# First MLP of a two-layer encoder step: hidden rows loaded one group ahead, and the conditioning of layer 1 in eight narrow and twelve wide steps

## The chip, the cores and the metric

One NeuronCore of a Trainium2 chip runs the kernel. TensorE (PE) multiplies matrices into eight PSUM banks of 128 x 512 f32, VectorE (DVE) and ScalarE (ACT) work on tiles of 128 partitions in SBUF and read PSUM, GpSimd (POOL) does little here, and SyncE (SP) issues the DMAs, which 16 DMA engines carry out. The metric is the device time of one execution in microseconds (us); less is better.

## The reference, cut to what matters

Two layers of an encoder work on 1024 prompt tokens and 32 sample tokens of width 1024. Each layer is a mixer and an MLP, each followed by a layer norm. Shifts, scales and gates (6 x 1024 a layer, and 2 x 1024 for the shared keys and values) come from a conditioning vector c for the prompt and another for the samples:

```python
def ada_mod(c, w, b):
    return jax.nn.silu(c) @ w + b
...
kv_shift, kv_scale = jnp.split(ada_mod(c, p['w_ada_kv'], p['b_ada_kv'])[:, None, :], 2, axis=-1)
...
x = layer_norm(ALPHA * x + (1 + g1) * y, p['ln_g'][l, 0], p['ln_b'][l, 0])
u = x * (1 + sc2) + sh2
f = jnp.square(jax.nn.relu(u @ p['w_up'][l])) @ p['w_down'][l]
x = layer_norm(ALPHA * x + (1 + g2) * f, p['ln_g'][l, 1], p['ln_b'][l, 1])
```

All is f32. The first MLP (layer 0) turns u (1056 tokens x 1024) into h (4096 wide) and that into f. What follows it is layer 1: q from the modulated x, then keys, values and attention.

## The kernel before, in words

Every f32 operand of a matmul is split into a high and a low part (fp32r, `split`, L89 on ACT and L90 on DVE), and a product is three matmuls (high x high, high x low, low x high: L118, L119, L120). Tokens lie along the free dimension, T = 1056, in three blocks `TBS` of 384, 384 and 288, or in four quarters `QN` of 264.

**Up.** `mlp7(L0)` first makes h. The 16 column blocks pb of w_up are worked on in `jobs`, a pair (pb, half of the tokens): 22 jobs of seven products each, 154 in all, and a product is 12 matmuls of 264 columns (`Seven.product`, L1269), evicted by ACT and DVE into H. `h_forms` squares and splits H (tile HL) and stores it to DRAM (`hpl`, L1136). The weights of a job come by `forms`: two raw tiles of 512 KB (rdn_u), four sums and eight splits on DVE and ACT. Raw tiles come from a ring of three buffers (tag raw, `raw_tile`), in which the weights of down (raw_dn) and the narrow conditioning data (rada) stand as well.

**Down.** h has 32 row blocks of 128, in eight groups g of four. A group takes four weight tiles pr (`w_plain`: raw_dn, split into w_dn), each for two column blocks fc of the output, and for each fc all token blocks: `dn_plain`, 12 matmuls into one PSUM bank, then an eviction by DVE that adds the gated product to the accumulator ACX (L1034). The part of a block that holds sample tokens is evicted on its own. Groups 0 to 6 go by fc, group 7 by token block, and after each of its blocks `L0.after` starts the layer norm of that block (`norm`, tasks n01_0 to n01_2). h of a group is loaded back by `h_load` (L1326, L1330), four tiles of 1056 KB: group 0 into half the tokens of U, whose contents are no longer needed, group 1 into four tiles hs of a pool f4 that takes the place of the H and HL tiles, group 2 into the other half of the tokens of U, and so on in turn. Where h lies in U in strips (groups 0, 2, 3, 5, 6), matmuls go by quarters of 264; in groups 1, 4 and 7 by TBS. `h_load(g + 2)` is called behind the second to fourth weight tile of group g.

**Conditioning beside the MLP.** Layer 1's conditioning is made by DVE while PE multiplies: for each slice of w_ada, 8 row blocks times a scalar of silu(c), for the prompt and for the samples, summed up (`aacc`, `aw`), then a transpose (`aat`, `awt`), a reduction (`cx`), and after every fourth narrow or second wide step a tiny matmul `adas`. `ada_cols` does it in narrow steps of two columns of 128 (two loads rada of 512 KB, 16 operations of 128 x 256, L238 and L241), `ada_wide` in wide steps of four (two loads radw of 1 MB into the ring wc of six buffers, where the split weights w_dn stand too; 16 operations of 128 x 512, L265 and L267). Both are generators: a `Flow` steps them by a nominal time, `flow.tick` is called after each product of up (QN / pace) and each block of down (n / 192), and a `yield x` asks for the next call after x. Up runs `ada_some`: 4 narrow steps for the first half of w_ada_kv at pace 480. Down runs `ada_rest`: 12 wide steps of w_ada[1], 2 wide steps of the second half of w_ada_kv, then the small `ada_fix` and `combine`, and `bias_table`. `L0.after` finishes all that is left (`flow.finish(norms["ada"])`) before it starts a norm.

**What sets the order.** The calls say what depends on what; a scheduler then fixes the order of each engine's instructions and of SP's DMAs, and at run time each engine takes its instructions strictly in that order. An order within an engine that was good for the scheduler's own guess of the times is kept whatever the real times are.

At pace 480 a product counts 264 / 480 = 0.55, so a narrow step with `ADA_B` = (4, 2, 1, 8) takes 8 + 4 products for each half and 2 at the end, 26; the fourth has 15 at its end, and they are done with product 3 x 26 + 24 + 15 = 117. At pace 320 a product counts 0.825, and a step takes 2 x (5 + 3) + 2 = 18; eight of them, with 10 at the end of the fourth and the eighth, come to 160, more than the 154 there are.

## Time and profile before

| | us |
|---|---|
| median of 3 runs | 2483.89 |
| the profiled execution | 2483.62 |
| its span, first to last instruction | 2481.8 |
| PE busy in the span | 2367.8 |
| DVE busy | 1994.5 |
| ACT busy | 1179.6 |

Times in the profile are counted from the start of the span. Up's seven products run from about 640 to 862 us; groups 0 to 7 of down begin at 862.2, 919.6, 966.5, 1013.4, 1060.5, 1107.3, 1154.2 and 1201.1; the first matmul of q is at 1295.14. PE's busy time counts a matmul until its modelled end, so PE can be busy without being at its peak. Where a line says `<-`, the name behind it is what the instruction waited for.

### The profile page before, as it was taken

How to read it: one execution, taken by the hardware profiler on the slowest of the kernel's cores; microseconds unless marked ns; L12 is line 12 of the kernel's file. 1: busy time of each engine (PE TensorE's matmuls, PEld its weight loads, DVE VectorE, ACT ScalarE, POOL GpSimd, SP SyncE). 2: the span in 40 equal slices, each digit the busy share in tenths (PEclk: the TensorE clock that was granted, in tenths of full speed). 3: DMA queues.
4: the chain of work that ended last, by engine and by line, in shares of the span. 5: the costliest groups of instructions: out<-in, count | busy, mean ns of one | idle time of the engine just before them, and what ended most of it. 6: DMA issues, size and time to landing. Idle time of an engine off the chain costs nothing.

```text
span 2481.8 us, 45295 instructions
## 1 busy us (share of the span) xinstructions
PE 2367.8 (95%) x17564; PEld 2274.1 (92%) x17564; DVE 1994.5 (80%) x4254; ACT 1179.6 (48%) x2394; POOL 167.0 (7%) x315
## 2 busy tenths in 40 slices
PE   7999999999999989999939989999999999899997
PEld 4999999999999989999939978779999999899997
DVE  4899999788787779998398666764998888888778
ACT  4644456487566611111038456762776777322212
POOL 0211100000000000000000224430000000000003
PEclk9999999999999999999969999999999999999999
DMA  8433224346556896574231330033376779966642
GB/s 295 123 109 101 84 88 131 115 136 210 181 191 226 300 349 234 202 243 138 88 101 65 98 79 1 10 79 77 123 267 226 256 255 344 368 234 239 227 163 71
DMA packets 298556, 423.68 MB, mean 171 GB/s; under 512 B 15832, under 2 KB 222060, under 8 KB 295268
## 3 DMA queue, kind: packets, MB, share of 16 engines
q1 hardware_dynamic: 298340, 420.78, 50.7%
q8 instruction: 138, 2.26, 0.4%
q14 instruction: 78, 0.64, 0.1%
HBM read 304.91 MB, written 118.17 MB: 170 GB/s over the span
## 4 chain that ended last, share of the span: by engine, by line
PE 46%; DVE 13%; DMA 5%; ACT 4%; issue 2%; SPq 1%; POOL 0%; DVEq 0%; ACTq 0%; POOLq 0%
PE dn L1407 11%; PE up L1269 5%; PE dn L120 5%; PE dn L118 5%; PE dn L119 5%; PE pv L1838 3%; PE s L1781 2%; PE pt L1816 2%; DVE wf_u L90 2%; DMA rdn_u<-in_w_up_dram 1%; PE q L118 1%; DVE HL L90 1%; PE q L119 1%; PE q L120 1%; PE op_b L118 1%
## 5 line engine op out<-in xcount | busy, mean ns | idle before, releaser
L1034 DVE SCALAR_TENSOR_TENSOR ACX<-dn,ada,ACX 128x264 f32<-128x264 f32 (+6 forms) x696 | 288.5, 437 | 122.9 <-PE dn L120 74.2
L1407 PE MATMUL dn<-fx,wf_d 128*128 128x264 f32 x2016 | 255.1, 286 | 6.1 <-DVE ACX L1034 3.8
L1407 PEld LDWEIGHTS dn<-fx,wf_d 128*128 128x128 f32 x2016 | 249.9, 189 | 8.1 <-DVE ACX L1034 2.4
L118 PE MATMUL dn<-U,w_dn 128*128 128x264 f32 x640 | 183.9, 287 | 6.0 <-DVE ACX L1034 6.0
L119 PE MATMUL dn<-U,w_dn 128*128 128x264 f32 x640 | 182.8, 286 | 0.0
L120 PE MATMUL dn<-U,w_dn 128*128 128x264 f32 x640 | 181.0, 285 | 1.5 <-DVE w_dn L90 1.5
L89 ACT CAST w_dn<-raw_dn 128x1024 fp32r<-128x1024 f32 x36 | 37.6, 1050 | 281.1 <-PE dn L120 125.3
L1269 PE MATMUL up<-TF,wf_u 128*128 128x264 f32 x1056 | 143.3, 285 | 2.1 <-ACT H L1272 2.1
L265 DVE SCALAR_TENSOR_TENSOR aw<-radw,cs,aw 128x512 f32<-128x512 f32 x196 | 138.9, 745 | 7.9 <-DMA radw<-in_w_ada_dram 7.9
L1269 PE MATMUL up<-u,wf_u 128*128 128x264 f32 x1056 | 139.6, 285 | 1.3 <-ACT wf_u L89 0.6
L1269 PE MATMUL up<-U,wf_u 128*128 128x264 f32 x1056 | 139.6, 285 | 1.1 <-ACT H L1272 0.5
L1269 PEld LDWEIGHTS up<-TF,wf_u 128*128 128x128 f32 x1056 | 134.2, 188 | 3.0 <-ACT H L1272 2.7
L1269 PEld LDWEIGHTS up<-U,wf_u 128*128 128x128 f32 x1056 | 133.1, 188 | 2.2 <-DVE H L1275 1.4
L1269 PEld LDWEIGHTS up<-u,wf_u 128*128 128x128 f32 x1056 | 132.6, 188 | 1.9 <-ACT wf_u L89 0.8
L118 PE MATMUL dn<-hs,w_dn 128*128 128x384 f32 (+2 forms) x416 | 131.9, 317 | 0.0
L119 PE MATMUL dn<-hs,w_dn 128*128 128x384 f32 (+2 forms) x416 | 131.3, 316 | 0.0
L120 PE MATMUL dn<-hs,w_dn 128*128 128x384 f32 (+2 forms) x416 | 130.7, 314 | 0.0
L118 PEld LDWEIGHTS dn<-U,w_dn 128*128 128x128 f32 x640 | 121.7, 190 | 6.4 <-DVE ACX L1034 6.2
L120 PEld LDWEIGHTS dn<-U,w_dn 128*128 128x128 f32 x640 | 120.3, 189 | 2.0 <-DVE w_dn L90 2.0
L119 PEld LDWEIGHTS dn<-U,w_dn 128*128 128x128 f32 x640 | 122.1, 191 | 0.0
L238 DVE SCALAR_TENSOR_TENSOR ada_room<-ada_room,cs 128x256 f32<-128x256 f32 x224 | 99.7, 480 | 3.3 <-DMA ada_room<-in_w_ada_dram 3.3
L120 PE MATMUL up<-u,w_up 128*128 128x264 f32 x320 | 92.4, 290 | 3.0 <-DVE w_up L90 3.0
(394 smaller groups left out, 7161.9 us busy)
## 6 DMA issues: line engine op xcount, KB each, us to landing
hpl<-HL SPq DMA_DIRECT2D x144, 264.0 KB
rdn_u<-in_w_up_dram SPq DMA_DIRECT2D x64, 512.0 KB
hd<-HL SPq DMA_DIRECT2D x28, 1056.0 KB
fx<-hd SPq DMA_DIRECT2D x50, 528.0 KB
radw<-in_w_ada_dram SPq DMA_DIRECT2D x24, 1024.0 KB
hd<-HM SPq DMA_DIRECT2D x28, 792.0 KB
U<-hpl SPq DMA_DIRECT2D x40, 528.0 KB
raw_up<-in_w_up_dram SPq DMA_DIRECT2D x40, 512.0 KB
```

Of the source, the lines that this page charges most:

```text
L90: (eng or nc.vector).tensor_sub(dst_l, src, dst_h.bitcast(F32))
L118: nc.tensor.matmul(ps, wh, mov(0, k), start=(k == 0), stop=False)
L119: nc.tensor.matmul(ps, wh, mov(1, k), start=False, stop=False)
L120: nc.tensor.matmul(ps, wl, mov(0, k), start=False, stop=(k == nk - 1))
L238: nc.vector.scalar_tensor_tensor(acc[:, cnd], raw[:, k], sc, acc[:, cnd], op0=ALU.mult, op1=ALU.add)
L265: nc.vector.scalar_tensor_tensor(acc[cnd], raw[:, k], sc, acc[cnd], op0=ALU.mult, op1=ALU.add)
L1034: nc.vector.scalar_tensor_tensor(xs, ps[:, off + o:off + o + mm_], gate[:, fc, cnd:cnd + 1], xs, op0=ALU.mult, op1=ALU.add)
L1269: nc.tensor.matmul(p, self.ws[w][:, wl, k], moving(f, tp, xl, k), start=first and k + n_ == 0, stop=k == 3 and n_ == 2, skip_group_check=n ...
L1407: nc.tensor.matmul(p, ws[w][:, wl, k], t[:, s0, xl], start=first and k + n_ == 0, stop=k == kg - 1 and n_ == 2, skip_group_check=not first)
L1781: nc.tensor.matmul(s[:, b, :w], qst, kk[i][:, g, k0 + j0:k0 + j0 + w], start=(i == 0), stop=(i == 1))
L1816: nc.tensor.transpose(pt[:kp, j - j0, pr * P:(pr + 1) * P], ps_[pr][:, j * P:j * P + kp], ident)
L1838: nc.tensor.matmul(pv[64 * e:64 * e + 64, :nq], V[:kp, vt0 + j, g * 64:(g + 1) * 64], pts[e][:kp, j, :nq], start=(j == 0), stop=(j == nt - 1))
```

## The change

- Groups 1 to 7 all go by TBS. Odd groups have h in the tiles of f4, even groups from 2 on in `L.half(c)`, the high half of U over all tokens; group 0 keeps its strips. `h_load(g + 1)` is called in group g, behind its first weight tile, for all four tiles at once; before it was `h_load(g + 2)`.
- `ada_some` has 8 narrow steps (all of w_ada_kv) at pace 320, `ada_rest` 12 wide ones. A wide step calls for the next half's load before it works on its own half, and yields (5, 5, 2) instead of (6, 3, 3).
- The norm of block 2 has shorter waits.

```diff
--- before.py
+++ after.py
@@ -251,22 +251,33 @@
 
     def ada_wide(src, c0, base, nch, mk, tmp_f, raw_f, step):
 
-        for j in range(0, nch, 4):
-            acc = [tmp_f([P, 512], f"aw_{base}_{j}_{cnd}") for cnd in range(2)]
-            for half in range(2):
-                raw = raw_f([P, 4, 512], f"radw_{base}_{j}_{half}")
-                nc.sync.dma_start(raw, src[512 * half:512 * half + 512, c0 + j * P:c0 + (j + 4) * P].rearrange(
+        jobs = [(j, half) for j in range(0, nch, 4) for half in range(2)]
+        raws = {}
+
+        def load(i):
+            if i < len(jobs):
+                j, half = jobs[i]
+                raws[i] = raw_f([P, 4, 512], f"radw_{base}_{j}_{half}")
+                nc.sync.dma_start(raws[i], src[512 * half:512 * half + 512, c0 + j * P:c0 + (j + 4) * P].rearrange(
                     "(k p) c -> p k c", p=P))
-                yield step[0]
-                for k in range(4):
-                    for cnd in range(2):
-                        sc = cs[:, 4 * half + k, cnd:cnd + 1]
-                        if half or k:
-                            nc.vector.scalar_tensor_tensor(acc[cnd], raw[:, k], sc, acc[cnd], op0=ALU.mult, op1=ALU.add)
-                        else:
-                            nc.vector.tensor_scalar(acc[cnd], raw[:, k], sc, None, op0=ALU.mult)
-                    if k == 1:
-                        yield step[1]
+        load(0)
+        yield step[0]
+        for i, (j, half) in enumerate(jobs):
+            load(i + 1)
+            raw = raws.pop(i)
+            if not half:
+                acc = [tmp_f([P, 512], f"aw_{base}_{j}_{cnd}") for cnd in range(2)]
+            for k in range(4):
+                for cnd in range(2):
+                    sc = cs[:, 4 * half + k, cnd:cnd + 1]
+                    if half or k:
+                        nc.vector.scalar_tensor_tensor(acc[cnd], raw[:, k], sc, acc[cnd], op0=ALU.mult, op1=ALU.add)
+                    else:
+                        nc.vector.tensor_scalar(acc[cnd], raw[:, k], sc, None, op0=ALU.mult)
+                if k % 2:
+                    yield step[k // 2]
+            if not half:
+                continue
             for cnd in range(2):
                 at = tmp_f([P, 512], f"awt_{base}_{j}_{cnd}")
                 nc.vector.transpose(at, acc[cnd])
@@ -859,11 +870,11 @@
         return acc
 
     ADA_B = (4.0, 2.0, 1.0, 8.0)
-    ADA_W = (6.0, 3.0, 3.0)
+    ADA_W = (5.0, 5.0, 2.0)
     NOW = True
     TAIL = (1.0, 1.5)
     W00 = (6.0, 12.0, 0.0, 0.0, 0.0, 3.0)
-    W01 = (6.0, 12.0, 3.0, 3.0, 3.0)
+    W01 = ((6.0, 12.0, 3.0, 3.0, 3.0), (3.0, 6.0, 0.0, 0.0, 0.0))
     W10 = ((10.0, 12.0, 0.0, 0.0, 0.0, 3.0), (16.0, 14.0, 0.0, 0.0, 0.0, 3.0))
 
     def make_layer(acc, pp, uo, cut=None):
@@ -1321,16 +1332,13 @@
         def h_load(g, c, hl=None):
 
             src = hpl[4 * order_p[g] + c]
-            if g % 3 == 1:
-                t = f4p.tile([P, 2, T], F32R, tag=f"f4{c}", name=f"hs_{l}_{g}_{c}")
-                nc.sync.dma_start(t.bitcast(F32), src)
-                hs_p[g, c] = lambda hl, t0, n: t[:, hl, t0:t0 + n]
+            if hl is not None:
+                nc.sync.dma_start(L.strips(2 * c + hl).bitcast(F32), src[:, hl].rearrange("p (h t) -> p h t", h=2))
+                hs_p[g, c] = lambda hl, t0, n: L.strips(2 * c + hl)[:, t0 // (2 * QN), t0 % (2 * QN):t0 % (2 * QN) + n]
                 return
-            for i in range(2) if hl is None else (hl,):
-                nc.sync.dma_start(L.strips(g % 3 // 2, 2 * c + i).bitcast(F32),
-                                  src[:, i].rearrange("p (h t) -> p h t", h=2))
-            hs_p[g, c] = lambda hl, t0, n: L.strips(g % 3 // 2, 2 * c + hl)[:, t0 // (2 * QN),
-                                                                            t0 % (2 * QN):t0 % (2 * QN) + n]
+            t = f4p.tile([P, 2, T], F32R, tag=f"f4{c}", name=f"hs_{l}_{g}_{c}") if g % 2 else L.half(c)
+            nc.sync.dma_start(t.bitcast(F32), src)
+            hs_p[g, c] = lambda hl, t0, n: t[:, hl, t0:t0 + n]
 
         def dn_plain(g, fc, t0, n):
             ps = mm(f"dn{l}_{g}_{fc}_{t0}")
@@ -1458,11 +1466,11 @@
                 if g < 7:
                     for pr in range(4):
                         w_plain(g, pr)
-                        if g < 6 and pr:
-                            for c in ((0, 1), (2,), (3,))[pr - 1]:
-                                h_load(g + 2, c)
+                        if g and pr == 0:
+                            for c in range(4):
+                                h_load(g + 1, c)
                         for fc in (2 * pr, 2 * pr + 1):
-                            for t0, n in TBS if g % 3 == 1 else blocks_p:
+                            for t0, n in TBS if g else blocks_p:
                                 dn_plain(g, fc, t0, n)
                 else:
                     for pr in range(4):
@@ -1560,11 +1568,10 @@
     h_cm.__exit__(None, None, None)
 
     def ada_some():
-        yield from ada_cols(a["w_ada_kv"], 0, 96, 8, mm, tmp_t, ADA_B)
+        yield from ada_cols(a["w_ada_kv"], 0, 96, 16, mm, tmp_t, ADA_B)
 
     def ada_rest():
         yield from ada_wide(a["w_ada"][1], 0, 48, 48, mm, tmp_t, wc_tile, ADA_W)
-        yield from ada_wide(a["w_ada_kv"], D, 104, 8, mm, tmp_t, wc_tile, ADA_W)
         ada_fix(48, [(1, "sc"), (2, "g"), (4, "sc"), (5, "g")])
         ada_fix(96, [(1, "sc")])
         combine(1, lng(1), lnb(1), ada_part(1, 1), ada_part(1, 0))
@@ -1574,7 +1581,7 @@
 
     class L0:
         wups = wup0
-        l, nw, pace, alloc, add, gate = 0, 0, 480, mm, add_gated_at, ada_part(0, 5)
+        l, nw, pace, alloc, add, gate = 0, 0, 320, mm, add_gated_at, ada_part(0, 5)
         blocks = TBS
         pairs, quarters = (0, 1), (0, 1, 2, 3)
         first = FIRST
@@ -1593,9 +1600,13 @@
             t0 = (2 * tp + q) * QN
             return L0.rows(4 * kap, 4, hl)[:, :, t0:t0 + QN]
 
-        def strips(tp, i):
-
+        def strips(i):
+
+            tp = L0.pairs[0]
             return L0.rows(2 * i % KC, 2, 2 * i // KC)[:, :, 2 * tp * QN:2 * (tp + 1) * QN]
+
+        def half(c):
+            return L0.rows(2 * c, 2, 0)
 
         def scratch(i):
             t = accp0.tile([P, 2, 2, KG, QN], F32R, tag=f"acc{i}", name=f"TF0_{i}")
@@ -1619,7 +1630,7 @@
             t0, n = blk
             ti = TBS.index(blk)
             flow.finish(norms["ada"])
-            norms[ti] = flow.add(norm(ti, 1, f"n01_{ti}", W01, False, lambda ti: acc_dma(
+            norms[ti] = flow.add(norm(ti, 1, f"n01_{ti}", W01[ti == 2], False, lambda ti: acc_dma(
                 xsp[1][:, :, t0:t0 + n], acc[ti], True)), now=NOW)
     mlp7(L0)
```

What this does to the order, at three places. In the rows below dn_g_fc_t names a block of down (group, column block, first token), radw_48_j_half a wide load, aw_104 the wide steps of w_ada_kv, n01_0 the norm of block 0, and the last numbers only count tiles.

SP in group 0, before:

```order
L96 DMA raw_dn0_0_2_10665<-in_w_down_dram 128x4x256
L96 DMA raw_dn0_0_3_10800<-in_w_down_dram 128x4x256
L1609 DMA ACX0_1_10391<-xsp3_80 128x2112 x2
L1136 DMA hpl0_6125<-HL0_15_1_10325 256x1x264 x4
L258 DMA radw_48_0_0_10431<-in_w_ada_dram 128x4x512
L1330 DMA U_134<-hpl0_6125 128x2x528
L1136 DMA hpl0_6125<-HL0_13_1_10394 256x1x264 x4
L1330 DMA U_134<-hpl0_6125 128x2x528 x2
L1326 DMA hs_0_1_0_10407<-hpl0_6125 128x2112
L1326 DMA hs_0_1_1_10409<-hpl0_6125 128x2112
L1326 DMA hs_0_1_2_10411<-hpl0_6125 128x2112
L1326 DMA hs_0_1_3_10413<-hpl0_6125 128x2112
```

and now:

```order
L261 DMA radw_48_0_0_10531<-in_w_ada_dram 128x4x512
L261 DMA radw_48_0_1_10590<-in_w_ada_dram 128x4x512
L1147 DMA hpl0_6125<-HL0_13_1_10490 256x1x264 x4
L261 DMA radw_48_4_0_10716<-in_w_ada_dram 128x4x512
L1340 DMA hs_0_1_0_10509<-hpl0_6125 128x2112
L1340 DMA hs_0_1_1_10511<-hpl0_6125 128x2112
L1340 DMA hs_0_1_2_10513<-hpl0_6125 128x2112
L1340 DMA hs_0_1_3_10515<-hpl0_6125 128x2112
L96 DMA raw_dn0_0_2_10765<-in_w_down_dram 128x4x256
L96 DMA raw_dn0_0_3_10902<-in_w_down_dram 128x4x256
L96 DMA raw_dn0_1_0_11031<-in_w_down_dram 128x4x256
```

The third and fourth weights of group 0 (raw_dn0_0_2, raw_dn0_0_3) stood ahead of the last stores of h, and now stand behind the four tiles of h of group 1.

DVE in group 7, before (block 2's evictions, the two wide steps, the norm of block 0):

```order
L1034 SCALAR_TENSOR_TENSOR ACX0_0_9705<-dn0_7_3_768_14367,ada_88,ACX0_0_9705 128x256
L1034 SCALAR_TENSOR_TENSOR ACX0_0_9705<-dn0_7_3_768_14367,ada_88,ACX0_0_9705 128x32
L267 TENSOR_SCALAR aw_104_0_0_13995<-radw_104_0_0_13997,cs_87 128x512
...
L274 TENSOR_REDUCE cx_118<-awt_104_0_1_14090 128x2x8
L267 TENSOR_SCALAR aw_104_4_0_14093<-radw_104_4_0_14095,cs_87 128x512
L267 TENSOR_SCALAR aw_104_4_1_14094<-radw_104_4_0_14095,cs_87 128x512
L265 SCALAR_TENSOR_TENSOR aw_104_4_0_14093<-radw_104_4_0_14095,cs_87,aw_104_4_0_14093 128x512
...
L274 TENSOR_REDUCE cx_118<-awt_104_4_1_14118 128x2x8
L915 TENSOR_TENSOR s_n01_0_14152<-ACX0_0_9705 128x768
L288 TENSOR_TENSOR ada_88<-adas_104_6_14121,pt2_86 128x16
L917 TENSOR_TENSOR s_n01_0_14152<-s_n01_0_14152,ACX0_1_10391 128x768
```

and now:

```order
L1045 SCALAR_TENSOR_TENSOR ACX0_1_10487<-dn0_7_6_0_13704,ada_88,ACX0_1_10487 128x384
L1045 SCALAR_TENSOR_TENSOR ACX0_1_10487<-dn0_7_7_0_13718,ada_88,ACX0_1_10487 128x384
L928 TENSOR_TENSOR s_n01_0_13732<-s_n01_0_13732,ACX0_1_10487 128x768
L929 TENSOR_TENSOR s_n01_0_13732<-s_n01_0_13732 128x384
L1045 SCALAR_TENSOR_TENSOR ACX0_0_9762<-dn0_7_0_384_13740,ada_88,ACX0_0_9762 128x384
L90 TENSOR_TENSOR sr_n01_0_13737<-s_n01_0_13732,sr_n01_0_13737 128x384
L1045 SCALAR_TENSOR_TENSOR ACX0_0_9762<-dn0_7_2_384_13768,ada_88,ACX0_0_9762 128x384
L936 TENSOR_TENSOR ACX0_0_9762<-ACX0_0_9762,mean_n01_0_13782 128x2x384 x2
L936 TENSOR_TENSOR ACX0_1_10487<-ACX0_1_10487,mean_n01_0_13782 128x2x384 x2
L940 TENSOR_TENSOR q0_n01_0_13786<-q0_n01_0_13786,q2_n01_0_13789 128x768
```

The norm's sums (s_n01_0) stood behind both wide steps and behind evictions of block 2 (tokens from 768); now they stand among the last evictions of block 0, ahead of those of block 1 (tokens from 384).

DVE at the end of up, before (H0_13 and H0_15 are evictions of the last two jobs, which PE waits for; wf_u0_13 is a weight split):

```order
L1275 TENSOR_TENSOR H0_13_1_10234<-up0_13_1_1_10262,H0_13_1_10234 128x264
L90 TENSOR_TENSOR w_dn0_0_0_10278<-raw_dn0_0_0_10276,w_dn0_0_0_10278 128x1024
L1275 TENSOR_TENSOR H0_15_1_10103<-up0_15_1_2_10215,H0_15_1_10103 128x264
L90 TENSOR_TENSOR wf_u0_13_6_10295<-rdn_u0_13_1_10059,wf_u0_13_6_10295 128x512
L90 TENSOR_TENSOR w_dn0_0_1_10348<-raw_dn0_0_1_10346,w_dn0_0_1_10348 128x1024
L1275 TENSOR_TENSOR H0_13_1_10234<-up0_13_1_0_10235,H0_13_1_10234 128x264
L90 TENSOR_TENSOR HL0_15_1_10325<-H0_15_1_10103,HL0_15_1_10325 128x4x264
```

and now:

```order
L1286 TENSOR_TENSOR H0_13_1_10319<-up0_13_1_1_10347,H0_13_1_10319 128x264
L1286 TENSOR_TENSOR H0_15_1_10178<-up0_15_1_2_10300,H0_15_1_10178 128x264
L238 SCALAR_TENSOR_TENSOR aacc_96_14_10129<-rada_96_14_1_10298,cs_87,aacc_96_14_10129 128x256 x8
L245 STREAM_TRANSPOSE aat_96_14_10439<-aacc_96_14_10129 128x512
L90 TENSOR_TENSOR w_dn0_0_0_10363<-raw_dn0_0_0_10361,w_dn0_0_0_10363 128x1024
L90 TENSOR_TENSOR wf_u0_13_6_10384<-rdn_u0_13_1_10134,wf_u0_13_6_10384 128x512
L90 TENSOR_TENSOR HL0_15_1_10414<-H0_15_1_10178,HL0_15_1_10414 128x4x264
L246 TENSOR_REDUCE cx_118<-aat_96_14_10439 128x16
L1286 TENSOR_TENSOR H0_13_1_10319<-up0_13_1_0_10320,H0_13_1_10319 128x264
```

The eviction H0_13 from bank 0 (up0_13_1_0) now has half a narrow step (aacc, aat, cx), the split of HL0_15 and the first weight split of down ahead of it.

## The prediction

> **What bounds the kernel now.** I read the busy times first, then busy time by stretch, then the waits of the first MLP's second half, then the timeline round the longest wait. The first line of the page:
>
> ```profile
> PE 2367.8 (95%) x17564; PEld 2274.1 (92%) x17564; DVE 1994.5 (80%) x4254; ACT 1179.6 (48%) x2394; POOL 167.0 (7%) x315
> ```
>
> TensorE (PE) is the bound almost everywhere: 2481.8 less 2367.8 leaves 114 us in which it does nothing. The change can gain only from that rest, or from a clock that it costs. By stretch (busy us and instructions of each engine, granted clock, DMA share, GB/s); the first two rows are the last part of up, the third is group 0 of down, then groups 1, 2 and 6, then group 7 and what follows it:
>
> ```profile
> 642.00:786.00 144.00, 142.52 (x1162) 141.43 (x1161) 117.82 (x219) 89.38 (x159) 0.00 (x0) 1.00 0.59 190
> 786.00:862.00 76.00, 74.04 (x607) 72.93 (x606) 56.86 (x94) 53.18 (x93) 0.00 (x0) 1.00 0.86 287
> 862.20:919.70 57.50, 50.01 (x387) 49.23 (x386) 37.03 (x72) 6.99 (x8) 0.00 (x0) 0.94 0.96 348
> 904.10:910.90 6.80, 5.48 (x22) 5.12 (x23) 6.28 (x15) 1.23 (x2) 0.00 (x0) 0.50 0.85 264
> 919.70:966.60 46.90, 46.90 (x298) 46.62 (x298) 45.26 (x81) 5.25 (x5) 0.00 (x0) 1.00 0.66 218
> 966.60:1013.50 46.90, 46.90 (x394) 46.73 (x393) 45.73 (x87) 4.19 (x4) 0.00 (x0) 1.00 0.66 237
> 1154.30:1201.10 46.80, 46.80 (x386) 46.80 (x385) 30.03 (x67) 4.68 (x5) 0.00 (x0) 1.00 0.38 120
> 1201.10:1242.80 41.70, 41.64 (x262) 41.12 (x260) 15.27 (x32) 0.00 (x0) 0.00 (x0) 1.00 0.20 65
> 1242.80:1295.10 52.30, 12.03 (x50) 10.75 (x50) 50.86 (x83) 13.33 (x18) 0.00 (x0) 0.59 0.24 80
> ```
>
> The reader should see three things. PE is full in the groups; in 1242.8 to 1295.1 it works 12 of 52 us, at 0.59 of the clock, while VectorE (DVE) is full. Just before, DVE had been idle for 26 of 41.7 us. And group 0 takes 57.5 us where the others take 46.9. The waits between 860 and 1300 us (in total, times, longest) say why:
>
> ```profile
> PE adas L285 <- DVE cx L274: 22.4, 1, 22.4
> DVE aw L265 <- DMA radw<-in_w_ada_dram: 7.9, 3, 7.3
> PE var_n L912 <- ACT qr_n L89: 7.5, 1, 7.5
> PE dn L118 <- DVE ACX L1034: 6.0, 1, 6.0
> PE mean_n L912 <- ACT sr_n L89: 5.7, 2, 4.1
> PE q L118 <- ACT U L359: 4.7, 1, 4.7
> PE dn L120 <- DVE w_dn L90: 1.5, 2, 1.2
> ```
>
> After group 7 PE waits 22.4 + 7.5 + 5.7 + 4.7 = 40.3 us: first for two wide steps, then for the norm of block 0, which stands behind them on DVE:
>
> ```profile
> 1218.51 0.62 DVE L1034 SCALAR_TENSOR_TENSOR ACX<-dn,ada,ACX 128x384 f32<-128x384 f32 x1 [1.49 <-PE dn L120]
> ...
> 1240.16 0.88 DVE L267 TENSOR_SCALAR aw<-radw,cs 128x512 f32<-128x512 f32 x2
> 1240.95 9.36 DVE L265 SCALAR_TENSOR_TENSOR aw<-radw,cs,aw 128x512 f32<-128x512 f32 x14
> ...
> 1252.60 0.88 DVE L267 TENSOR_SCALAR aw<-radw,cs 128x512 f32<-128x512 f32 x2
> ...
> 1265.04 0.95 DVE L915 TENSOR_TENSOR s_n<-ACX 128x768 f32<-128x768 f32 x1
> ...
> 1295.14 1.33 PE L118 MATMUL q<-U,w_q 128*128 128x384 f32 x3 [4.73 <-ACT U L359]
> ```
>
> A wide step takes 1252.60 - 1240.16 = 12.4 us of DVE. Block 0 was complete at 1218.51 (first row: the eviction that ends it), its norm began at 1265.04, and the first matmul of q came 30.1 us later.
>
> **The change part by part.** *The tail.* The change has no wide step here: twelve remain, and by its order the last of them stands in the first blocks of group 6, so nothing is ahead of the norm of block 0. It starts when that block's last eviction is done. PE would have ended group 7 in 46.9 us; before, the first q matmul came 1295.14 - 1201.1 = 94.0 us after the group's start. In the new order two blocks of other columns stand ahead of the second half of block 0 (0.62 + 1.49 = 2.1 us for one of 384 columns by the first row, so 1.6 for one of 288), with a wait of about 1.5 us for the low half of the third weights (an estimate from the row of the same wait, 1.5 in 2 times). Block 0 was complete 1219.1 - 1201.1 = 18.0 us into the group, and is now at 18.0 + 5.2 = 23.2. The norm then needs what it needed before, 30.1 us, with these differences, all on DVE:
>
> ```profile
> L1034 DVE SCALAR_TENSOR_TENSOR ACX<-dn,ada,ACX 128x384 f32<-128x384 f32 x16 | 9.9, 617 | 22.4 <-PE dn L120 22.4
> L90 DVE TENSOR_TENSOR w_q<-raw_q,w_q 128x1024 fp32r<-128x1024 f32 x5 | 6.1, 1218 | 0.0
> L1034 DVE SCALAR_TENSOR_TENSOR ACX<-dn,ada,ACX 128x256 f32<-128x256 f32 x7 | 3.4, 482 | 4.1 <-PE dn L120 4.1
> L1034 DVE SCALAR_TENSOR_TENSOR ACX<-dn,ada,ACX 128x32 f32<-128x32 f32 x8 | 1.9, 243 | 0.0
> ```
>
> Some 8 us of evictions of blocks 1 and 2 fall into it (8 x 0.62 + 4 x 0.73), and four of the five q weight splits (4.9 us) fall out of it. So q starts 53 us into the group if the differences cancel, 56 if all of them count, and 51 if the two sums of s_n that the new order puts ahead of the last eviction (0.95 each) save their time: 94.0 less that is a gain of 38 to 43 us. The best possible is PE's own end (94.0 - 46.9 = 47), the worst a norm stretched by all evictions without relief (94.0 - 61 = 33). I take **-41**, the middle, since DVE is full through the old stretch (50.86 of 52.3) and this is a sum of DVE's work. The norms of blocks 1 and 2 stay beside the q matmuls, as now.
>
> *Up, last part.* Four narrow steps come in. Narrow steps between 642 and 862 us on DVE:
>
> ```profile
> L238 DVE SCALAR_TENSOR_TENSOR aacc<-rada,cs,aacc 128x256 f32<-128x256 f32 x56 | 23.9, 478 | 4.1 <-DMA rada<-in_w_ada_kv_dram 4.1
> L245 DVE STREAM_TRANSPOSE aat<-aacc 128x512 f32<-128x512 f32 x4 | 2.8, 707 | 0.1
> L246 DVE TENSOR_REDUCE cx<-aat 128x16 f32<-128x512 f32 x4 | 2.7, 681 | 0.1
> L241 DVE TENSOR_SCALAR aacc<-rada,cs 128x256 f32<-128x256 f32 x6 | 1.8, 349 | 1.8 <-DMA rada<-in_w_ada_kv_dram 1.8
> ```
>
> That is 31.2 / 4 = 7.8 us a step. A product is 12 matmuls of 144 / 1162 = 0.124 us, 1.49 us. At pace 480 a step takes 26 products (38.7 us, a fifth of DVE), and four of them end at the 117th of 154 products; at pace 320 it takes 18 (26.8 us, 29%), and eight of them last to the end. DVE is at 82% in the first stretch, which becomes 82 - 20 + 29 = 91%: it hides them. It is at 75% in the second, where none ran: 104%, or 3 us too much. PE's wait for DVE in all of this part was small:
>
> ```profile
> PE up L1269 <- DVE H L1275: 0.5, 2, 0.2
> ```
>
> So a lag may vanish in the PSUM banks (0); but the weight forms of the last jobs have no cover left (+12, the second rival). I take **+4**, nearest to the 3 us.
>
> *Group 0.* Its wait before was for conditioning data: one radw load was issued behind the four h tiles of group 1 (SP's queue, then DVE):
>
> ```profile
> 872.49 2.55 SPq L1136 DMA_DIRECT2D hpl<-HL  x4
> ...
> 876.60 2.59 SPq L1326 DMA_DIRECT2D hs<-hpl  x4
> ...
> 879.95 0.48 SPq L258 DMA_DIRECT2D radw<-in_w_ada_dram  x1
> ```
>
> ```profile
> 889.15 0.49 DVE L1034 SCALAR_TENSOR_TENSOR ACX<-dn,ada,ACX 128x264 f32<-128x264 f32 x1 [1.58 <-PE dn L120]
> 896.98 5.39 DVE L265 SCALAR_TENSOR_TENSOR aw<-radw,cs,aw 128x512 f32<-128x512 f32 x8 [7.33 <-DMA radw<-in_w_ada_dram]
> ```
>
> What is issued after the h tiles lands after them: 17 us from issue to use. In the new order that place is taken by the third and fourth weights of group 0, which before went out ahead of everything; narrow data now holds the raw buffer that they use. They go out at about 880, behind a radw load and four h tiles: 1024 + 4 x 1056 + 512 KB = 5.9 MB from 875.0 on, at the 348 GB/s of the group's row 17 us, so 892; the cast and the split follow, and DVE has fourteen conditioning operations (about 8.5 us at the rate of the wide step above) queued ahead of the split, behind an eviction at 885.8: ready at about 896. PE needs them at half the group, 862.2 + 23.5 = 885.7. So it waits 10 us instead of 1.5 + 6.0. After the 6.0 us wait the clock stood at 0.50 for 6.8 us, which cost 3.4: 13.4 against the 57.5 - 46.9 = 10.6 that group 0 loses now: **+3**. Bounds: -10.6 (the weights come in time) and +9 (another radw load and the rest of a wide step ahead).
>
> The Trainium skill, "TensorE: Matmul & The Clock Gate", section "What's actually happening", says that the clock is halved after one idle window of about 3.4 us and is full again after one busy window of that length. The row agrees that 6.0 us of idling is enough, but has two windows at half, not one. By the page a wait costs 1.7 us instead of 3.4, the term +1, and the sum 2447.
>
> *Wider blocks and loads.* Group 1 (blocks of 384, 384, 288) takes the 46.9 us that group 2 takes with blocks of 264; four groups gain nothing that this view shows: **-0.5** (0 to -2). Two wide steps and eight evictions a group fewer leave DVE 42 to 44 us of work a group by the new order and these durations, against 45.7 busy in group 2, so PE stays the bound. h one group ahead: four tiles are 4.3 MB, 12 us at 348 GB/s, needed 47 us later; hidden, and if not, the slower rival. The next group's first weights are read ahead of them in SP's queue.
>
> *Sum.* The profiled execution took 2483.62 us (span 2481.8 and 1.8 round it), 0.3 under the median of 2483.89. 2483.6 - 41 + 4 + 3 - 0.5 = **2449 us**, 1.4% less. About 2% is what a measurement of this kernel can tell from no change.
>
> **The rivals.** *Better:* the up part hides all, and group 0's weights land in time: -4, and -13.6 at most, so 2431 to 2440. For it: PE lost so little in up. Against it: the new order of SP's queue.
>
> *Up is bound by its weights:* the narrow data keeps one of three raw buffers to the end, the up weights have two, and each of the last three jobs waits for its 1 MB (3.7 us at 287 GB/s): +11 instead of +4, and with a slow group 0 (+9) 2457 to 2470.
>
> *The wide steps are not done in time,* so that the change doesn't do what it says: two left behind cost 2 x 12.4 = 25 us again, 2474. Against it: 12 were done by group 6 before, with 97% of DVE used.
>
> *Slower:* h comes at the start of the group ahead, 4.3 MB in one burst, and the radw loads wait behind it. Then DVE stands as it did for 7.3 us in group 0, and PE loses 6.0 + 3.4 = 9.4 us a group. Four of the six groups decide it (+38 against -35); all six give 2505. Against it: before, too, four h tiles went out together at the start of groups, and all other waits of DVE for radw add up to 7.9 - 7.3 = 0.6 us.
>
> **How the numbers follow.** Forecast (2440 to 2459) 0.62; better 0.14; up bound by weights 0.12; wide steps late 0.05; slower 0.04; others 0.03. The predicted time is 2449. The range 2431 to 2470 takes in the first three cases and leaves out some 0.13. Faster by over 2% is below 2434, half of the better case and a little more: 0.10. Slower by over 2% is above 2533, more than six stalled groups: 0.03. Within 2%: 0.87.
>
> **What would show it.** In the profile after: no wait of adas for cx at the end and no DVE operation on aw after group 6; q starting 50 to 57 us after group 7's start; one PE wait of 8 to 12 us in the middle of group 0, for w_dn, with half clock behind it; groups 1 to 6 at 47 us each; DVE over 95% busy in the last 60 us of up, with PE waits of 2 to 6 us there. I am wrong if the groups take more than 48 us, if q starts later than 60 us into the group, or if up ends more than 10 us later than at 862.2.

## The result and the profile after

The changed kernel takes 2473.16 us (median of 6 runs, 2469.87 to 2474.31) against 2484.05 before (median of 6 as well, one of which took 5875.08 us): a ratio of 0.9955, 95% interval 0.9942 to 0.9969. It is faster by about 11 us, where 35 were forecast, and the interval, 0.13% to either side, tells that from no change. Its profiled execution has a span of 2471.5 us. The first line of its page, and the stretches that answer to those of before (busy us and instructions of PE, PEld, DVE, ACT, POOL; granted clock, DMA share, GB/s): two of up, group 0, the half-clock part of group 0, groups 1 and 6, group 7 up to the first matmul of q, and q up to the first matmul of kv.

```profile
PE 2371.9 (96%) x17180; PEld 2273.6 (92%) x17180; DVE 1993.4 (81%) x4254; ACT 1181.9 (48%) x2394; POOL 165.4 (7%) x315
```

```profile
642.00:786.00 144.00, 141.67 (x1151) 140.82 (x1151) 122.78 (x234) 87.05 (x153) 0.00 (x0) 0.99 0.60 193
786.00:880.50 94.50, 80.58 (x614) 76.53 (x613) 78.01 (x149) 55.13 (x95) 0.00 (x0) 0.98 0.79 253
880.50:944.70 64.20, 53.24 (x417) 52.48 (x418) 56.56 (x109) 11.22 (x13) 0.00 (x0) 0.89 0.84 298
918.60:924.80 6.20, 6.18 (x28) 6.09 (x29) 4.19 (x5) 2.09 (x2) 0.00 (x0) 0.52 1.05 380
944.70:991.50 46.80, 46.80 (x298) 46.52 (x297) 45.10 (x80) 4.21 (x4) 0.00 (x0) 1.00 0.68 240
1178.60:1225.40 46.80, 46.80 (x298) 46.52 (x297) 21.78 (x51) 5.25 (x5) 0.00 (x0) 1.00 0.58 201
1225.40:1277.40 52.00, 48.24 (x296) 47.37 (x294) 39.78 (x62) 12.14 (x17) 0.00 (x0) 1.00 0.17 51
1277.40:1382.50 105.10, 98.67 (x582) 96.27 (x583) 78.65 (x146) 70.56 (x147) 5.87 (x3) 0.97 0.28 88
```

q of the kernel before, for the last row:

```profile
1295.10:1394.00 98.90, 97.15 (x582) 95.50 (x583) 77.87 (x142) 70.29 (x147) 6.93 (x3) 0.98 0.26 83
```

Read by stage, each boundary against that of before:

| stage | before | after | difference | forecast |
|---|---|---|---|---|
| up, until group 0 starts | 862.2 | 880.5 | +18.3 | +4 |
| group 0 | 57.5 | 64.2 | +6.7 | +3 |
| groups 1 to 6 | 281.4 | 280.7 | -0.7 | -0.5 |
| group 7's start to the first q | 94.0 | 52.0 | -42.0 | -41 |
| first q to first kv | 98.9 | 105.1 | +6.2 | 0 |

They sum to -11.5. What follows kv has the same order in both kernels, and so has what stands ahead of up's seven products; the span ends 10.3 us earlier. These two unchanged parts show how far one profile can differ from the next: over the twelve profiles here up's first product starts between 630.0 and 634.0, and what follows the first kv takes 1084.2 to 1091.8 us. Here it starts at 633.45 instead of 630.95, so 2.5 us of the first row were lost before up began. In group 0's stretch PE makes 30 matmuls more than before (417 against 387): two products of up that are delayed into it (24 matmuls, 3.0 us) and eight tiny ones of adas, with 0.9 us of waits for them. So up itself lost some 20 us (18.3 - 2.5 + 4) and group 0 itself 3. The gain came as forecast; up took half of it away, and q 6 us more.

What PE and the weights' splits wait for in the last part of up (786 to 880.5 us; in total, times, longest):

```profile
PE up L1280 <- ACT wf_u L89: 6.1, 5, 2.6
DVE s_u L1244 <- DMA rdn_u<-in_w_up_dram: 5.9, 3, 2.9
ACT wf_u L89 <- DMA rdn_u<-in_w_up_dram: 6.6, 8, 1.9
PE up L1280 <- DVE wf_u L90: 3.1, 6, 1.1
```

PE waits for the weights' splits, and these for the raw weights. Why the raw weights are late is seen when SP's queue and DVE are laid side by side. The loads of two weight pairs and of the narrow data on SP, where a row gives the issue:

```profile
841.42 0.37 SPq L231 DMA_DIRECT2D rada<-in_w_ada_kv_dram  x1
...
843.83 0.37 SPq L1228 DMA_DIRECT2D rdn_u<-in_w_up_dram  x1
...
850.95 0.37 SPq L1228 DMA_DIRECT2D rdn_u<-in_w_up_dram  x1
...
860.72 5.97 SPq L1228 DMA_DIRECT2D rdn_u<-in_w_up_dram  x2
```

The narrow work on DVE at the same time:

```profile
845.55 1.67 DVE L238 SCALAR_TENSOR_TENSOR aacc<-rada,cs,aacc 128x256 f32<-128x256 f32 x4 [0.21 <-DMA rada<-in_w_ada_kv_dram]
...
847.49 1.27 DVE L238 SCALAR_TENSOR_TENSOR aacc<-rada,cs,aacc 128x256 f32<-128x256 f32 x3
...
850.45 0.48 DVE L238 SCALAR_TENSOR_TENSOR aacc<-rada,cs,aacc 128x256 f32<-128x256 f32 x1
...
864.62 1.66 DVE L238 SCALAR_TENSOR_TENSOR aacc<-rada,cs,aacc 128x256 f32<-128x256 f32 x4
```

The second load of the first pair goes out at 850.95, 7 us behind the first; DVE ended the last operation of a narrow half step at 850.45 + 0.48 = 850.93. The second load of the next pair ends its issue at 860.72 + 5.97 = 866.69 and takes 0.37, so it began at 866.3; DVE ended its half step at 864.62 + 1.66 = 866.28. The load waits for the raw buffer that the narrow data holds: both go out within 0.05 us of the end of a half step. The ring has three buffers, taken in turn.

### The profile page after: what moved, and what is told of

The parts are those of the page before. It is cut to its first block, busy times and chain, and to the rows that moved or that the text cites. A ratio compares the mean times of both kernels' runs of the same rounds, so it can differ in the third digit from the quotient of the medians.

```text
span 2471.5 us, 44497 instructions
## 1 busy us (share of the span) xinstructions
PE 2371.9 (96%) x17180; PEld 2273.6 (92%) x17180; DVE 1993.4 (81%) x4254; ACT 1181.9 (48%) x2394; POOL 165.4 (7%) x315
## 4 chain that ended last, share of the span: by engine, by line
PE 65%; DVE 15%; DMA 8%; ACT 4%; issue 3%; POOL 1%; SPq 0%; DVEq 0%; ACTq 0%; POOLq 0%
PE dn L1415 11%; PE up L1280 7%; PE dn L118 5%; PE dn L119 5%; PE dn L120 5%; PE pv L1849 3%; PE s L1792 2%; PE pt L1827 2%; DVE wf_u L90 2%; DMA rdn_u<-in_w_up_dram 2%; PE up L120 2%; PE up L118 2%; PE up L119 2%; DVE HL L90 1%; PE op_a L118 1%
## 5 line engine op out<-in xcount | busy, mean ns | idle before, releaser
L1045 DVE SCALAR_TENSOR_TENSOR ACX<-dn,ada,ACX 128x264 f32<-128x264 f32 (+6 forms) x664 | 281.8, 448 | 115.0 <-PE dn L120 68.6
L118 PE MATMUL dn<-hs,w_dn 128*128 128x384 f32 (+2 forms) x512 | 161.4, 315 | 0.7 <-DVE ACX L1045 0.7
L120 PE MATMUL dn<-hs,w_dn 128*128 128x384 f32 (+2 forms) x512 | 160.3, 313 | 1.3 <-DVE w_dn L90 1.3
L119 PE MATMUL dn<-hs,w_dn 128*128 128x384 f32 (+2 forms) x512 | 161.0, 315 | 0.0
L1280 PE MATMUL up<-U,wf_u 128*128 128x264 f32 x1056 | 145.8, 290 | 15.8 <-ACT wf_u L89 6.8
L118 PE MATMUL dn<-U,w_dn 128*128 128x384 f32 (+2 forms) x416 | 130.8, 315 | 10.2 <-ACT w_dn L89 10.0
L119 PE MATMUL dn<-U,w_dn 128*128 128x384 f32 (+2 forms) x416 | 130.9, 315 | 0.0
L120 PE MATMUL dn<-U,w_dn 128*128 128x384 f32 (+2 forms) x416 | 129.5, 313 | 0.0
L274 DVE SCALAR_TENSOR_TENSOR aw<-radw,cs,aw 128x512 f32<-128x512 f32 x168 | 118.9, 744 | 0.0
L120 PEld LDWEIGHTS dn<-hs,w_dn 128*128 128x128 f32 x512 | 96.4, 188 | 1.7 <-DVE w_dn L90 1.7
L118 PEld LDWEIGHTS dn<-hs,w_dn 128*128 128x128 f32 x512 | 96.3, 188 | 1.1 <-DVE ACX L1045 1.0
L119 PEld LDWEIGHTS dn<-hs,w_dn 128*128 128x128 f32 x512 | 96.5, 188 | 0.0
```

The costliest lines, as they stand in the source:

```text
L118: nc.tensor.matmul(ps, wh, mov(0, k), start=(k == 0), stop=False)
L119: nc.tensor.matmul(ps, wh, mov(1, k), start=False, stop=False)
L120: nc.tensor.matmul(ps, wl, mov(0, k), start=False, stop=(k == nk - 1))
L274: nc.vector.scalar_tensor_tensor(acc[cnd], raw[:, k], sc, acc[cnd], op0=ALU.mult, op1=ALU.add)
L1045: nc.vector.scalar_tensor_tensor(xs, ps[:, off + o:off + o + mm_], gate[:, fc, cnd:cnd + 1], xs, op0=ALU.mult, op1=ALU.add)
L1280: nc.tensor.matmul(p, self.ws[w][:, wl, k], moving(f, tp, xl, k), start=first and k + n_ == 0, stop=k == 3 and n_ == 2, skip_group_check=n ...
```

## Experiments

Three theories of the loss in up: *ring* (the narrow data holds a raw buffer, as just read), *DVE* (31 us more work there), *DMA* (4 MB more traffic). Each run was timed against the kernel before on the same chip.

### 1. Narrow data in buffers of its own

```diff
-yield from ada_cols(a["w_ada_kv"], 0, 96, 16, mm, tmp_t, ADA_B)
+yield from ada_cols(a["w_ada_kv"], 0, 96, 16, mm, tmp_t, (3.0, 3.0, 1.0, 8.0), L0.nar)
...
+L.nar = lambda shape, name: hhp.tile(shape, F32, tag="nar", name=name, bufs=3)
...
-for half in range(2):
-    raw = raw_f([P, 4, 256], f"rada_{base}_{j}_{half}")
+for q in range(4):
+    raw = raw_f([P, 2, 256], f"rada_{base}_{j}_{q}")
...
+if not NW:
+    flow.finish()
 hh_cm.__exit__(None, None, None)
```

> The changed kernel, with the narrow data of up in buffers of its own (three of 256 KB, four loads a step in place of two of 512 KB) and no longer in the ring of three raw buffers. Same DVE work, same bytes. Ring theory (the narrow data holds a raw buffer, and the second load of each weight pair waits until a narrow half step is done): group 0 starts at 863 to 868 us instead of 880.5, and the third weight of group 0 goes out ahead of the h tiles, so the time is 2450 to 2460. DVE theory (31 us more work on DVE delays the splits) and DMA theory (4 MB more traffic in up): group 0 starts at 877 us or later, time 2467 to 2476.

Measured: 2445.38 us, ratio 0.9841 (0.9826 to 0.9856); group 0 starts at 861.2. The last five jobs of the changed kernel, then those of this one, from the start of the first to the last matmul of up:

```profile
814.90:887.70 72.80, 59.82 (x452) 55.92 (x451) 60.60 (x118) 41.54 (x70) 0.00 (x0) 0.98 0.82 272
```

```profile
806.90:865.80 58.90, 55.89 (x454) 54.47 (x452) 57.34 (x108) 38.92 (x66) 0.00 (x0) 1.00 0.88 293
```

And its loads on SP:

```profile
825.48 0.37 SPq L1243 DMA_DIRECT2D rdn_u<-in_w_up_dram  x1
827.86 0.37 SPq L1243 DMA_DIRECT2D rdn_u<-in_w_up_dram  x1
...
837.89 0.37 SPq L1243 DMA_DIRECT2D rdn_u<-in_w_up_dram  x1
840.26 0.37 SPq L1243 DMA_DIRECT2D rdn_u<-in_w_up_dram  x1
```

The two loads of a pair are 2.4 us apart instead of 7.1. DVE is busy for 57.34 of 58.9 us, 97%, and PE waits only 3.0 us in all (24 matmuls of group 0 lie in this stretch too): DVE hides the four steps, as the prediction had hoped, and so does DMA at 0.88. The result is better than the ring theory's own bands. From up's first product to group 0 it took 231.3 us before, 245.9 to 248.4 in the changed kernel and the runs with its order of up (4, 5, 8), and 227.9 to 231.7 in all runs with buffers of their own (1, 6, 7, 9, 10). This settles it for the ring against the sums of DVE's and DMA's work. The run also loads in quarters and spreads the operations of a half step (waits of 3, 3 for 4, 2), and does not test these alone; that it is the buffer is read from the two loads above.

### 2. The same loads with less DVE work

```diff
-nc.vector.scalar_tensor_tensor(acc[:, cnd], raw[:, k], sc, acc[:, cnd], ...)
+nc.vector.scalar_tensor_tensor(acc[:, cnd, :16], raw[:, k, :16], sc, acc[:, cnd, :16], ...)
```

> The changed kernel, in which 14 or 15 of the 16 narrow operations of a step work on 16 of 256 columns (part of the conditioning is left out): about 0.4 us less for each, some 44 us less DVE work in up. Loads and the order of the buffers stay. Ring theory: the buffers are freed at the same places of the program, so most of the loss stays, group 0 starts at 872 to 881 us, time 2463 to 2473. DVE theory: the loss goes, group 0 starts by 866 us, time 2450 to 2458.

Measured: 2463.68 us, 0.9917 (0.9902 to 0.9932); group 0 at 873.4, so 11 of the 18 us stay. The relief was smaller than supposed, since an operation of 16 columns still takes 0.23 us against 0.48 for 256:

```profile
L239 DVE SCALAR_TENSOR_TENSOR aacc<-rada,cs,aacc 128x16 f32<-128x16 f32 x110 | 17.9, 229 | 9.7 <-DMA rada<-in_w_ada_kv_dram 9.7
```

That is 110 x 0.25 = 28 us less DVE work, more than three of the four added steps (31 us). Start and time lie in the bands of the ring theory. The ring is the larger part; that shorter operations give the buffer back sooner fits the 7 us that went.

### 3. The narrow steps early

`pace` 320 becomes 200.

> The changed kernel with pace 200 for 320 in up: the eight narrow steps end before the last five jobs, which need new weights every 10.4 us. Ring theory: the last five jobs run as before the change, the first part of up loses 3 to 8 us more because DVE has a step every 19 us there; group 0 starts at 866 to 873 us, and its third and fourth weights go out ahead of the h tiles (58 to 61 us for the group instead of 64); time 2452 to 2464. DVE theory: the same work is pressed into less time, the loss stays or grows, group 0 starts at 880 us or later, time 2467 to 2480.

Measured: 2468.86 us, 0.9942 (0.9919 to 0.9964); group 0 starts at 885.3. Start and time lie in the bands of the DVE theory, but both halves of the expectation are seen. The last five jobs run as before the change (52.8 us; 53.4 before). The first seventeen end 24 us later (832.7 against 809.0), and the wait there is another one (waits from 642 to 833 us, then DVE at the longest of them):

```profile
PE up L1280 <- DVE H L1286: 15.5, 8, 5.0
```

```profile
699.23 3.25 DVE L238 SCALAR_TENSOR_TENSOR aacc<-rada,cs,aacc 128x256 f32<-128x256 f32 x8 [0.30 <-DMA rada<-in_w_ada_kv_dram]
702.40 0.68 DVE L90 TENSOR_TENSOR wf_u<-s_u,wf_u 128x512 fp32r<-128x512 f32 x1
...
704.79 1.10 DVE L1286 TENSOR_TENSOR H<-up,H 128x264 f32<-128x264 f32 x3
```

Eight narrow operations in one go (3.25 us) and what follows them stand ahead of three evictions of H, and PE waits 5.0 us for these. Here the cost is DVE's order, not its sum. So the ring explains the loss of the changed kernel, and the DVE theory holds where the steps are pressed together.

### 4. The conditioning part alone

The kernel before with `ada_some`, `ada_rest`, `ada_wide`, `ADA_W` and `pace` of the change; h, blocks and `W01` as they were.

> The kernel before with only the conditioning part of the change (eight narrow steps at pace 320, twelve wide ones, loads half a step early); h is loaded as before, and the blocks and the waits of block 2's norm are as before. If conditioning is all that matters: up as in the changed kernel (group 0 at 879 to 882 us), q 50 to 55 us after group 7's start, time 2470 to 2477. If h one group ahead in whole tiles was needed to let the wide steps through: groups 1 to 6 over 47.5 us or a wide step left at the end, time 2480 to 2500.

Measured: 2474.67 us, 0.9960 (0.9945 to 0.9975); group 0 at 877.3, q 52.0 us after group 7's start. Gain and loss both come from the conditioning part; loading h one group ahead is not needed for it. The parts of this part (the work moved into up, the loads half a step early, the other yields) were not run one by one.

### 5 and 6. Group 0's weights ahead of the h tiles

```diff
 L.down()
+for pr in (2, 3):
+    w_plain(0, pr)
 for c in range(4):
     h_load(1, c)
```

Group 0 of the changed kernel waits as forecast, for weights that SP issues behind a radw load and four h tiles (SP's queue, then PE):

```profile
898.42 0.67 SPq L261 DMA_DIRECT2D radw<-in_w_ada_dram  x1
899.13 3.15 SPq L1340 DMA_DIRECT2D hs<-hpl  x4
902.32 9.29 SPq L96 DMA_DIRECT2D raw_dn<-in_w_down_dram  x3
```

```profile
918.62 0.59 PE L118 MATMUL dn<-U,w_dn 128*128 128x264 f32 x1 [10.03 <-ACT w_dn L89]
```

> The changed kernel, with the third and fourth weight tiles of group 0 called for ahead of the four h tiles of group 1. If group 0's wait of 10 us comes from their place behind the h tiles: no wait for w_dn over 2 us in group 0, and 48 to 52 us for the group instead of 64.2 (880.5 to 944.7), time 2458 to 2465. If the wait only passes on to the radw loads, which now stand behind the h tiles, and DVE holds up PE's evictions as it did before: a PE wait of 5 to 8 us at dn for ACX, the group takes 55 to 60 us, time 2464 to 2470.

> The narrow data in buffers of its own (as in the first run) and the third and fourth weights of group 0 ahead of the h tiles. Up as in the first run (group 0 at 860 to 863 us). If the place in the queue was the cause: group 0 takes 47 to 52 us instead of 56.4, time 2436 to 2442. If the wait passes on to radw: 55 us or more, time 2443 to 2448.

Measured: 2468.58 us, 0.9933 (0.9917 to 0.9950), and with buffers of its own 2444.16, 0.9837 (0.9823 to 0.9852), which is not told apart from run 1. In run 5 group 0 takes 51.9 us instead of 64.2 and groups 1 to 6 take 288.2 instead of 280.7: the group came out as in the first branch, the time as in the second. Groups 0 and 1 of run 6:

```profile
858.50:906.90 48.40, 48.40 (x406) 48.17 (x405) 37.32 (x77) 8.20 (x9) 0.00 (x0) 1.00 0.92 335
906.90:961.00 54.10, 50.17 (x298) 49.08 (x297) 51.49 (x93) 4.20 (x4) 0.00 (x0) 0.94 0.63 226
```

Group 0 falls from 56.4 to 48.4 us, and group 1 rises from 46.8 to 54.1: there PE waits 3.63 us for the low half of group 1's first weight, and runs at half clock behind it. ACT, then DVE, on that weight:

```profile
901.00 1.06 ACT L89 CAST w_dn<-raw_dn 128x1024 fp32r<-128x1024 f32 x1 [28.51 <-DMA raw_dn<-in_w_down_dram]
```

```profile
909.30 2.73 DVE L289 SCALAR_TENSOR_TENSOR aw<-radw,cs,aw 128x512 f32<-128x512 f32 x4
...
912.47 1.22 DVE L90 TENSOR_TENSOR w_dn<-raw_dn,w_dn 128x1024 fp32r<-128x1024 f32 x1
```

Its load stands behind the h tiles and four radw loads and lands at 901; ACT makes the high half at once, but in DVE's order the low half stands behind conditioning, 10 us later. The wait went neither away nor to radw data, as the two branches had it, but to the next weight.

### 7. The q weights' low parts on POOL

`wblock` of the q weights with `nc.gpsimd`, in the kernel of run 6.

> As the run before, with the low parts of the q weights (128x1024) made by POOL instead of DVE: seven or eight operations of about 1.2 us leave DVE in group 7 and in q. If q is 6 us longer than before the change (105.1 for 98.9 us from the first matmul of q to the first of kv) because DVE must make the norms of blocks 1 and 2 beside it: 100 to 103 us, and 2 to 5 us less time than the run before, 2433 to 2440. If DVE's load is not the reason, or POOL's slower operation makes the weights late: the same or more, 2438 to 2446.

Measured: 2447.68 us, 0.9849 (0.9834 to 0.9863). q is 106.6 us as in run 6, and starts 55.0 instead of 52.0 us into group 7. POOL takes 2.63 us for what DVE does in 1.22:

```profile
L90 POOL TENSOR_TENSOR w_q<-raw_q,w_q 128x1024 fp32r<-128x1024 f32 x7 | 18.4, 2630 | 120.0 <-ACT w_q L89 120.0
```

Nor was DVE relieved of the 8.5 us that left it. While POOL works on w_q, three operations of the norms take 2.6 to 3.1 us instead of 0.55 and 0.95, and each ends 0.4 to 0.9 us behind POOL's; operations that read PSUM keep their times (ACX<-ACX,mean_n at 1244.40, 0.94 us). One of the three (POOL, then DVE; in run 6 it took 0.55):

```profile
1246.50 2.39 POOL L90 TENSOR_TENSOR w_q<-raw_q,w_q 128x1024 fp32r<-128x1024 f32 x1 [0.96 <-ACT w_q L89]
```

```profile
1246.54 2.77 DVE L968 TENSOR_TENSOR w_n<-w_n 128x384 f32<-128x384 f32 x1
```

The one at 1237.89 (2.59 us) and this one stand ahead of q: 4.2 us more, less the split of 1.22 us that left DVE there, are the 3 us by which q starts later. PE waits nowhere for w_q. So the run did not take DVE's load away, and does not acquit DVE.

### 8. The old waits in block 2's norm

`W01[ti == 2]` becomes `W01[0]`.

> The changed kernel with the old waits in the norm of block 2 too. If these shorter waits do not matter: q 103 to 107 us, time within 2 us of the changed kernel, 2471 to 2475. If they make q longer: 99 to 101 us, 2466 to 2470. If they were needed: 108 us or more, 2476 or more.

Measured: 2468.10 us, 0.9931 (0.9916 to 0.9946), an interval that overlaps the changed kernel's only at its end; q takes 102.7 us, between the bands, and the rest of the difference lies in up and group 0, where the order is the same, so it is not the waits' doing. In all kernels with the old waits q takes 102.7 to 103.8 us (runs 4, 8, 9, 10), in all with the new ones 104.8 to 106.7. The shorter waits cost some 2 us of q.

### 9. All of it mended

Runs 6 and 8 together, and in the second weight tile of group 0:

```diff
 w_plain(g, pr)
+if g == 0 and pr == 1:
+    w_plain(1, 0)
```

> Narrow data in buffers of its own, third and fourth weights of group 0 ahead of the h tiles, the first weight of group 1 called for in the second weight tile of group 0 (by the order three weights of group 1 now stand ahead of three radw loads that they followed), and the old waits in the norm of block 2. If the wait at the start of group 1 (3.6 us and half clock, 54.1 for 46.9 us) comes from the place of its weights behind five radw loads: groups 0 and 1 take 96 to 98 us together instead of 102.5, q is 102 to 104 us instead of 105 to 106.6, time 2434 to 2439. If the wait passes on once more, to DVE's radw data in groups 1 and 2: 102 us or more for groups 0 to 1 or a wait in group 2, time 2440 to 2446.

Measured: 2436.51 us, 0.9815 (0.9801 to 0.9830), the fastest of all. Groups 0, 1 and 2:

```profile
863.70:912.10 48.40, 48.40 (x406) 48.17 (x405) 37.31 (x77) 8.21 (x9) 0.00 (x0) 1.00 0.94 343
912.10:961.00 48.90, 47.27 (x298) 46.66 (x297) 47.72 (x87) 4.20 (x4) 0.00 (x0) 1.00 0.62 223
961.00:1007.80 46.80, 46.80 (x298) 46.52 (x297) 44.99 (x81) 5.25 (x5) 0.00 (x0) 1.00 0.62 224
```

The two groups take 97.3 us instead of 102.5, and q 103.4 instead of 106.6: 8.4 us, and the medians differ by 7.7. That this fits so well is in part luck, since the first matmul of q comes at 1247.0 in both runs: up, in the same order, ended 5.2 us later in run 9, and what follows kv, in the same order too, took 5.0 us less. The wait at group 1 came from the place of its first weight, and went no further. The weight's load moved ahead of three radw loads, and its low half moved ahead in DVE's order (it starts at 900.87 instead of 912.47); the run moves both and does not tell them apart.

### 10. Own buffers, h as before

Run 4 with the buffers of run 1.

> The kernel before with the conditioning part of the change alone and the narrow data in buffers of its own; h loaded as before (two groups ahead, in strips and whole tiles in turn). If the h part does little, as in the changed kernel (2473 with it, 2475 without): 2443 to 2449. If h one group ahead matters once up has no wait, for the weights of group 0 or the radw loads: 2450 to 2458.

Measured: 2452.08 us, 0.9872 (0.9856 to 0.9889), against 0.9841 with h one group ahead: q starts at 1256.0 instead of 1250.3 us, 4.0 of these 5.7 lost in group 0 (60.4 against 56.4) and 1.2 in groups 1 to 6. Once up does not wait, h one group ahead is worth some 5 us by these two stages; the two intervals only touch.

## Why the prediction was wrong

- **The tail was right.** -41 forecast, -42.0 measured; q 53 us into the group forecast, 52.0 measured. No wide step is left: the last sum into aw starts at 1178.0, just before group 6, and the last transpose of it ends at 1183. PE's waits from 1225.4 to the first q are 0.7, 1.3 and 1.7 us instead of 40.3.
- **Up failed, and with it the sum.** The step that failed is "I take **+4**, nearest to the 3 us". It was sized by DVE's load: 104%, 3 us too much. Run 1 has this load and loses nothing: group 0 starts at 861.2. The price lay in the raw ring, at some 20 us. The prediction had the mechanism as a rival with 0.12 and priced it at +11, "each of the last three jobs" waiting for one load. (Its upper end, 2470, does not follow from its terms: +11 for +4 and +9 for +3 give 2462.) Two things were missed. Each of the last five jobs has weights of its own, so there a pair of loads is due every 7 x 1.49 = 10.4 us. And the wait is not for the load's 3.7 us but for the narrow half step: 7.1 us between two loads of a pair, where they are 2.4 apart with own buffers. The five jobs took 72.8 us instead of 53.4, with 20 more matmuls of group 0 among theirs (2.5 us), so 3.4 each.
- **"DVE over 95% busy in the last 60 us of up" did not come**: 60.60 of 72.8 us is 83%. That row says that the sum of DVE's work is not the bound; that its order can still hold PE up is what run 3 shows.
- **Group 0 was right in place and size**: +3 forecast and measured, once what is left of up in it is taken off; the wait is 10.0 us as forecast, for the weights behind the h tiles, with 6.2 us at half clock behind it.
- **The groups were right**: 46.8 us each, -0.7 for -0.5. The slower rival, h bursts that delay radw in six groups, did not come: PE has no wait there, although DVE was as busy as before (45.10 of 46.80).
- **q was left out.** "The norms of blocks 1 and 2 stay beside the q matmuls, as now" put nothing in the sum, and q took 6.2 us more. The same operations of the norms stand behind q's first matmul in both kernels, and two of the eight q weight splits more than before (2.4 us). What changed is DVE's order: with its shorter waits the norm of block 2 overtakes that of block 1, its means and squares stand ahead of block 1's w_n, and PE waits 3.8 us for block 1's U (PE, then DVE):

```profile
1312.55 0.96 PE L118 MATMUL q<-U,w_q 128*128 128x384 f32 x4 [3.81 <-ACT U L370]
```

```profile
1298.67 2.75 DVE L936 TENSOR_TENSOR ACX<-ACX,mean_n 128x576 f32<-128x576 f32 x4
...
1308.63 0.56 DVE L951 SCALAR_TENSOR_TENSOR w_n<-var_n,w_n 128x384 f32<-128x384 f32 x1 [0.47 <-ACT w_n L950]
...
1310.79 2.69 DVE L955 TENSOR_TENSOR ACX<-ACX,w_n 128x768 f32<-128x768 f32 x3
```

  In run 8, with the old waits, this w_n starts 22.5 us after q's first matmul instead of 31.2, and PE's longest wait in q is 1.4 us:

```profile
1297.35 0.56 DVE L951 SCALAR_TENSOR_TENSOR w_n<-var_n,w_n 128x384 f32<-128x384 f32 x1
```

  That is some 2 us of the 6.2. The cause of the rest stays open: in run 8 PE still waits 3.6 us in q, against 1.6 before the change, and run 7 could not test DVE's load.

## What to carry to other kernels

When work is moved into a stage, count the buffers that it holds there and for how long, not only the engine time: a tile that is held over several steps in a ring that another stream takes in turn holds up that stream's loads at its own pace. Look for the part of the stage that turns over the ring fastest; it decides, not the average. When two tasks share an engine in a fixed order, a shorter nominal wait in one can put it ahead of what the other engine needs first. Work that is taken from one engine and given to another is not saved before the trace shows it: look whether the operations that stay grow longer. And a load that is moved ahead in one queue moves the next one behind something; what run 6 gained in group 0 it lost in group 1, until run 9 moved that too.

## What the runs showed of the hardware

Short waits cost the clock too. In the changed kernel the granted clock changes on a fixed grid of 3.41 us: it falls to half at 695.84, 856.27 and 1279.52, among others, which are 47 and 124 steps apart, and comes back one step later. Below are the stretches of the grid before and after the first two halvings. The first holds two waits of PE, of 0.63 and 0.90 us, the third one of 2.62 us. The last two rows share a single wait of 1.46 us, from 1289.03 to 1290.49:

```profile
692.43:695.84 3.41, 1.88 (x13) 1.46 (x12) 2.37 (x4) 2.30 (x4) 0.00 (x0) 1.00 0.03 10
695.84:699.25 3.41, 3.41 (x18) 3.41 (x17) 3.41 (x6) 2.55 (x6) 0.00 (x0) 0.50 0.50 156
852.86:856.27 3.41, 0.79 (x7) 0.58 (x6) 2.09 (x3) 2.31 (x3) 0.00 (x0) 1.00 0.36 124
856.27:859.68 3.41, 3.15 (x13) 2.85 (x14) 3.41 (x7) 2.58 (x5) 0.00 (x0) 0.50 0.74 245
1286.34:1289.76 3.42, 2.70 (x16) 2.38 (x14) 3.42 (x4) 0.58 (x1) 0.00 (x0) 1.00 0.73 209
1289.76:1293.17 3.41, 2.68 (x15) 2.64 (x16) 2.74 (x6) 2.92 (x5) 0.00 (x0) 1.00 0.86 270
```

1.5 us of idling in one stretch (PE busy for 1.88 of 3.41) were enough for 3.4 us at half clock, a loss of 1.7 us, more than the waits themselves; a single wait of 1.46 us, which the grid cuts in two, cost nothing. So two halvings in up are 3.4 of its 20 us. In these traces the busy share of a fixed stretch goes with the halving, not the length of a wait: in all twelve profiles, behind their first 4 us, no stretch at full clock with PE busy for over 0.62 of it was followed by a halving, and each with less than 0.44 was (worked out from the clock's times and PE's busy time). The prediction read two stretches at half clock behind the 6.0 us wait as two busy ones; in the first, 904.08 to 907.49, PE was busy for only 2.30 us.

The Trainium skill, "TensorE: Matmul & The Clock Gate", section "What's actually happening", has the halving come after an idle window of about 3.4 us; these rows show it after less.
